# The last three feature tiles of an FFN down projection, column tile by column tile; two PSUM banks begun first instead of four

## The chip, the cores and the metric

The kernel runs on one NeuronCore of one Trainium2 chip. The metric is the device time of one execution in microseconds (us), as the median over several executions. A core has a matmul engine (PE in the profile), three engines for elementwise work (DVE, the vector engine; ACT, the scalar engine; POOL, GpSimd) and SP, an engine that does nothing here but issue DMAs. Each engine takes its instructions strictly in the order in which they stand in its own stream; an instruction that has to wait holds up everything behind it on its engine. That holds for SP too: a DMA whose buffer isn't free yet holds up the DMAs behind it. Matmul results go into eight accumulator banks (PSUM); everything else lies in on-chip buffers (SBUF).

## The reference

One layer of a decoder trunk: attention and a state space model side by side, an output projection, and a gated FFN with a short convolution, then a final norm. It is run on a prompt of 2048 tokens and on 8 samples of 4 tokens (2080 tokens together), all in float32. What matters here is the last part, with D_MODEL = 1024 and D_FF = 2688:

```python
def _conv_ffn(h, prev, w_up, conv_w, conv_b, w_down):
    up = h @ w_up
    buf = jnp.concatenate([prev.astype(up.dtype), up], axis=1)
    c = conv_b + sum(conv_w[i] * buf[:, i:i + L] for i in range(CONV_W))
    a, g = jnp.split(c, 2, axis=-1)
    return (jax.nn.silu(g) * a) @ w_down, buf[:, -(CONV_W - 1):]
...
    x = x + f
...
    y_prompt = _rmsnorm(xp, norm_final)
    y_sample = _rmsnorm(xs, norm_final)
```

The change touches the product with `w_down`, the addition of `x`, and the norm behind it.

## The kernel before

**Stages.** After the mixer the FFN runs twice, for two token groups (`gi` = 0 with tokens 0 to 1023, `gi` = 1 with 1024 to 2079). In each, 21 calls of `unit` make the up projection, convolution and gate of one feature tile of 128 features each and write the result, as a high and a low part, to a scratch array `actscr` in DRAM. Then `down(gi, beside)` multiplies with `w_down`. `down` of group 0 is followed by the units of group 1.

**Tiles of down.** `TILESD` cuts group 0 into two token tiles of 512 and group 1 into three of 448, 352 and 256. Tiles are named here by their first token: 0, 512, 1024, 1472, 1824. For each, the output is 8 column tiles `m` of 128 columns, each accumulated in a PSUM bank of its own (`dn_<tile>_<m>`), over 21 feature tiles `f`. One pass of the loop handles one feature tile for all 8 columns. The inner step `one(i, m)` is `mm3`, three matmuls into bank m: high weights by high activations (L89), high weights by low activations (L90), low weights by high activations (L91). So a pass is 24 matmuls and a token tile 504.

**Weights.** `load_wd` reads the 128 x 1024 weights of a feature tile from DRAM (`wdr`, L1457, two raw buffers for even and two for odd feature tiles). ACT then casts the high part (`wdh`, L83) and POOL makes the low part by subtraction (`wdl`, L84). `wdh` and `wdl` have three buffers each, so the split of one feature tile can't begin before the matmuls of the third last one have read theirs. The units share these buffers: their weights (`whv`/`wlv`, `whs`/`wls`, `whg`/`wlg`) rotate through the same three. In group 1 the first 14 feature tiles stay in SBUF (`wd`) for all three token tiles; the last two token tiles run through the features in the order 0, 1, 14, 2, 3, 15, ..., 12, 13, 20, so only every third pass needs a split.

**Activations.** `load_a` reads the two parts of a feature tile (`ah`, `al`, L1475) from `actscr`, up to three tiles ahead, into ten buffers that the norm's squares (`sq_fo`) share.

**The end of a token tile.** Behind the 21 passes stands, for each column, a DMA that reads `x` (`xo`, L1519) and a DVE addition of the bank to it (L1522). Then `finish` takes the squares on ACT (L130, L133), adds them up on DVE (`ss_fo`, L134), sums over partitions with a matmul (`st_fo`, L1437), and goes by ACT (L1440, L1441) and DVE (L1442 to L1444) to the scale, to the multiplication (L1447) and the write of the output (L1448). `finish` is a generator: its second part, from `st_fo` on, is emitted within the next token tile.

**Which banks start first.** At the start of a tile some banks are still read by earlier work. `behind` names the columns that are left out of the first `wait` passes and put into `late`; at pass `wait` the `st_fo` of the tile before and then the late steps are emitted. For the first tile of a group `behind` is (2, 3, 6, 7) and `wait` is 2, for the others (7,) and 3. Banks 0 to 3, 4 and 5, and 6 and 7 belong to three kinds of PSUM pools that the units use too.

**What sets the order.** The program is written once, and a scheduler puts each engine's instructions in order, by dependencies and priorities. SP's stream holds the weight loads, the `ah`/`al` loads, the `xo` loads and the output writes of all this.

Of the kernel before, what the change touches and what calls it, by code (L numbers as in the profile page):

```python
# [27 lines left out]
NF = DFF // P  # L28
# [11 lines left out]
TILES3 = [(260 * i, 260) for i in range(8)]  # L40
CB = 10
TILESD = [[(0, 512), (512, 512)], [(1024, 448), (1472, 352), (1824, 256)]]
DLATE, ULATE = 3, 2
YB = 1
FINLOW = -35
HP = 0
# [40 lines left out]
def mm3(nc, ps, w, x, first, last):  # L87

    nc.tensor.matmul(ps, w[0], x[0], start=first, stop=False)  # L89
    nc.tensor.matmul(ps, w[0], x[1], start=False, stop=False)  # L90
    nc.tensor.matmul(ps, w[1], x[0], start=False, stop=last)  # L91
# [565 lines left out]
def body(tc, a):  # L657
# [16 lines left out]
    with ExitStack() as top:  # L674
# [756 lines left out]
        def finish(t0, n, xs, first):  # L1431

            with after_preload() if first else nullcontext():
                ss = sumsq(c, DP, xs, n, f"fo_{t0}", nc.vector)
            yield
            ps = psv[1].tile([P, 512], F32, tag="u3", name=f"st_fo_{t0}")[:, :n]
            nc.tensor.matmul(ps, ones[1024], ss, start=True, stop=True)  # L1437
            r0 = DP.tile([P, n], F32, "ss", f"r0_fo_{t0}")
            r = DP.tile([P, n], F32, "rs", f"rs_fo_{t0}")
            nc.scalar.activation(r0, ps, AF.Ln, bias=c.eps)  # L1440
            nc.scalar.activation(r0, r0, AF.Exp, scale=-0.5)  # L1441
            nc.vector.scalar_tensor_tensor(r, ps, EPS, r0, ALU.add, ALU.mult)  # L1442
            nc.vector.scalar_tensor_tensor(r, r, -0.5, r0, ALU.mult, ALU.mult)
            nc.vector.scalar_tensor_tensor(r, r, 1.5, r0, ALU.add, ALU.mult)  # L1444
            for k, x in enumerate(xs):
                with tc.high_priority(offset=FINLOW):
                    nc.vector.scalar_tensor_tensor(x, x, g_fin[:, k : k + 1], r, ALU.mult, ALU.mult)  # L1447
                nc.sync.dma_start(yv[:, k, t0 : t0 + n], x)  # L1448
# [3 lines left out]
        def load_wd(gi, j, t0):  # L1452

            if j in wds:
                return wds[j]
            r = (sp if j % 2 else wp).tile([P, KD, P], F32, tag="wur", name=f"wdr_{t0}_{j}", bufs=2).rearrange("p k n -> p (k n)")
            nc.sync.dma_start(r, a["w_down"][j * P : j * P + P, :])  # L1457
            if gi and j < 14:
                if j in (4, 5):
                    w = [ffn.hc.tile([P, D], F32R, tag=f"t2{j - 4}{i}", name=f"wd{i}_{j}") for i in "hl"]  # L1460
                else:
                    i = j if j < 4 else j - 6
                    pl, nm = ((ha, "x0"), (hd, "q1"), (hb, "q0"))[0 if j < 4 else 1 + i // 4]
                    t = pl.tile([P, 2, D], F32R, tag=f"{nm}{i % 4 // 2}{'hl'[i % 2]}", name=f"wd_{j}")
                    w = [t[:, 0], t[:, 1]]
                wds[j] = w
            else:
                w = [wp.tile([P, KD, P], F32R, tag=f"wu{i}", name=f"wd{i}_{t0}_{j}", bufs=3).rearrange("p k n -> p (k n)") for i in "hl"]
            ffn.last_act, ffn.last_pool = split(nc, *w, r, nc.scalar, nc.gpsimd)
            return w  # L1470

        def load_a(j, t0, n):
            hl = [dt([P, n], F32R, f"a{i}_{t0}_{j}") for i in "hl"]
            for i, t in enumerate(hl):
                ffn.last_sp = nc.sync.dma_start(t.bitcast(F32), actscr[:, j, 1 - i, t0 : t0 + n]).ins  # L1475
            return hl

        def down(gi, beside):

            old = None  # L1480
            for ti, (t0, n) in enumerate(TILESD[gi]):
                xs, pts, ahl, late = [], {}, {}, []
                order = list(range(NF))
                if gi and ti:
                    order = [f for i in range(7) for f in (2 * i, 2 * i + 1, 14 + i)]

                def one(i, m):
                    if m not in pts:
                        pl, tag = ((psx, "ux"), (psu, "u2"), (psv[0], "u3"), (psv[1], "u3"))[max(0, m - 2) // 2 if m < 6 else m - 4]
                        pts[m] = pl.tile([P, 512], F32, tag=tag, name=f"dn_{t0}_{m}")  # L1490
                    mm3(nc, pts[m][:, :n], [w[:, m * P : m * P + P] for w in ahl[i][1]], ahl[i][0], i == 0, i == NF - 1)

                hls = {} if ti else ffn.first
                for i, j in enumerate(order):
                    for ahead in range(i, min(i + 3, NF)):
                        if ahead not in hls:
                            hls[ahead] = load_a(order[ahead], t0, n)
                    ahl[i] = hls[i], load_wd(gi, j, t0)
                    if ti == 0:
                        behind, wait = (2, 3, 6, 7), ULATE  # L1500
                    else:
                        behind, wait = (KD - 1,), DLATE
                    for m in range(KD):
                        if i < wait and m in behind:
                            late.append((i, m))
                        else:
                            if i == wait and late:
                                if old is not None:
                                    next(old, None)
                                for li, lm in late:  # L1510
                                    one(li, lm)
                                late = []
                            one(i, m)
                    if i > (0, 5)[ti > 0]:
                        with tc.issue_after(ffn.last_dve), tc.issue_after(ffn.last_act), tc.issue_after(ffn.last_pool), tc.issue_after(ffn.last_sp):
                            next(beside, None)
                for m in range(KD):
                    x = xp.tile([P, 2 * W], F32, tag="xo", name=f"xo_{t0}_{m}", bufs=8)[:, :n]
                    nc.sync.dma_start(x, x2scr[:, m, t0 : t0 + n])  # L1519
                    xs.append(x)  # L1520
                    with tc.high_priority(offset=HPD):
                        nc.vector.tensor_tensor(x, x, pts[m][:, :n], ALU.add)  # L1522
                old = finish(t0, n, xs, ti == 0)
                next(old)
            return old
# [17 lines left out]
        for gi in range(2):  # L1543
            ffn.first = {}
            for j in range(NF):
                if (gi, j) != (0, 0):
                    ws = load_wup(gi, j)
                unit(gi, j, ws, None if j or gi else finish_front, (last_norm if gi else None) if j == 0 else load_ahead if j == NF - 1 else None)
            beside = prepare(1) if gi == 0 else iter(())
            last = down(gi, beside)  # L1550
            for _ in beside:
                pass
# [125 lines left out]
```

## Time and profile before

| | us |
|---|---|
| median of 3 runs | 2178.76 (2177.89 to 2179.62) |
| the profiled execution, its own time | 2182.85 |
| span of the profile | 2180.4 |
| mean granted PE clock of the profiled execution | 0.976 |

The five token tiles of `down` stand in this execution at 1199.0, 1319.1, 1897.7, 2012.1 and 2101.1 us from the span's start (the first matmul of the tile, or where it would have come). The windows view gives for these stretches:

```profile
core 0: us, PE busy (x) PEld busy (x) DVE busy (x) ACT busy (x) POOL busy (x), PEclk, DMA share, GB/s
1199.00:1319.00 120.00, 118.50 (x506) 94.19 (x504) 58.20 (x83) 45.61 (x67) 63.94 (x32) 1.00 0.84 274
1319.00:1451.00 132.00, 123.00 (x510) 96.84 (x509) 38.74 (x39) 28.59 (x34) 58.80 (x27) 0.97 0.64 214
1897.70:2012.00 114.30, 107.39 (x506) 97.25 (x504) 12.59 (x28) 23.80 (x35) 39.08 (x17) 0.96 0.58 165
2012.00:2101.00 89.00, 84.14 (x508) 82.99 (x507) 18.97 (x27) 12.78 (x19) 17.34 (x7) 0.98 0.52 171
2101.00:2180.00 79.00, 62.38 (x510) 60.45 (x508) 24.49 (x46) 11.12 (x20) 12.43 (x5) 0.94 0.41 120
```

A row of this view is a stretch of time, its length, the busy time and the number of instructions of each engine, and PEclk, the mean clock granted to PE. A row of the timeline is the start, the duration (of several like instructions in a row, together), engine, line, operation and tiles; behind it in square brackets stands how long the engine had been idle before and what ended that (the releaser). A row of the view of waits is who waited for what: the sum in us, how many times, the longest.

### The profile page before, as it was taken

To read this page: it belongs to the slowest core of one execution; us is meant where nothing else is said; L and a number is where in the kernel's file an instruction comes from. 1 tells how busy PE (TensorE), PEld (TensorE's weight loads), DVE (VectorE), ACT (ScalarE), POOL (GpSimd) and SP (SyncE) were. 2 spreads that over 40 slices of the span, in tenths; PEclk is the share of its full clock that TensorE was granted. 3 is DMA by queue.
4 is the path that set the end of the run, shared out by engine and by line. 5 is a ranking of instruction groups with operands and counts; after the bars stand their busy time and mean duration, and the time that the engine had idled before them with its cause. 6 is when DMAs were issued, how large, how long until landed. Compare 5 with 4: busy or idle time off the path is not lost.

```text
span 2180.4 us, 41454 instructions
## 1 busy us (share of the span) xinstructions
PE 2051.2 (94%) x14685; PEld 1922.0 (88%) x14685; DVE 1297.7 (60%) x3295; ACT 1055.7 (48%) x2467; POOL 1217.6 (56%) x1199
## 2 busy tenths in 40 slices
PE   8989999978999979999999998999999999999997
PEld 7977878867999979999999786779999999888997
DVE  8849898368566576676766265246666666601231
ACT  6625554675444456666666332235665665612011
POOL 4777676334456766666665553455666666823120
PEclk9999999989999989999999999999999999999999
DMA  7854434786578733333334885924333333573643
GB/s 230 255 195 135 137 103 119 144 230 190 150 240 273 247 118 96 110 108 101 110 101 127 269 275 193 315 84 158 108 101 105 108 97 109 179 201 125 197 140 92
DMA packets 290319, 347.58 MB, mean 159 GB/s; under 512 B 41896, under 2 KB 246320, under 8 KB 289584
## 3 DMA queue, kind: packets, MB, share of 16 engines
q1 hardware_dynamic: 290112, 344.94, 51.7%
q8 instruction: 116, 1.90, 0.4%
q14 instruction: 91, 0.75, 0.1%
HBM read 232.70 MB, written 107.80 MB: 156 GB/s over the span
## 4 chain that ended last, share of the span: by engine, by line
PE 76%; DVE 7%; DMA 6%; POOL 5%; ACT 3%; issue 2%; SPq 1%; DVEq 0%; POOLq 0%; ACTq 0%
PE ux L1365 20%; PE u L1365 16%; PE dn L90 7%; PE dn L91 7%; PE dn L89 7%; PE wo L90 2%; PE wo L89 2%; PE wo L91 2%; PE qkv L89 2%; PE qkv L91 2%; PE qkv L90 2%; PE o L570 1%; DVE xo L1447 1%; DMA wdr<-in_w_down 1%; PE tp_b L559 1%
## 5 line engine op out<-in xcount | busy, mean ns | idle before, releaser
L84 POOL TENSOR_TENSOR wdl<-wdr,wdh 128x1024 fp32r<-128x1024 f32 x65 | 159.4, 2457 | 279.5 <-ACT wdh L83 242.4
L89 PE MATMUL dn<-ah,wdh 128*128 128x512 f32 (+3 forms) x552 | 204.4, 370 | 7.6 <-DMA ah<-actscr 3.6
L91 PE MATMUL dn<-ah,wdl 128*128 128x512 f32 (+3 forms) x552 | 203.7, 369 | 2.5 <-POOL wdl L84 2.5
L90 PE MATMUL dn<-al,wdh 128*128 128x512 f32 (+3 forms) x552 | 204.0, 370 | 0.7 <-DMA al<-actscr 0.7
L1330 ACT ACTIVATE cc<-u,cw 128x260 f32<-128x260 f32 (+1 forms) x252 | 141.5, 563 | 97.3 <-DVE u L1408 67.1
L1522 DVE TENSOR_TENSOR xo<-xo,dn 128x512 f32<-128x512 f32 (+3 forms) x40 | 21.9, 584 | 262.3 <-PE dn L91 262.2
L83 ACT CAST wdh<-wdr 128x1024 fp32r<-128x1024 f32 x65 | 68.1, 1050 | 224.9 <-PE dn L90 183.6
L84 POOL TENSOR_TENSOR wls<-s,whs 128x1024 fp32r<-128x1024 f32 x42 | 101.0, 2406 | 132.9 <-ACT whs L83 132.9
L1331 DVE SCALAR_TENSOR_TENSOR cc<-u,cw,cc 128x260 f32<-128x260 f32 (+1 forms) x252 | 121.1, 481 | 66.1 <-ACT cc L1330 64.6
L89 PE MATMUL wo<-mh,wo 128*128 128x260 f32 x512 | 148.4, 290 | 0.0
L90 PE MATMUL wo<-ml,wo 128*128 128x260 f32 x512 | 146.3, 286 | 0.1
L91 PE MATMUL wo<-mh,wo 128*128 128x260 f32 x512 | 146.2, 286 | 0.0
L1408 DVE TENSOR_TENSOR u<-u,cb 128x262 f32<-128x262 f32 x84 | 36.5, 435 | 159.2 <-PE u L1365 159.2
L89 PEld LDWEIGHTS dn<-ah,wdh 128*128 128x128 f32 x552 | 104.3, 189 | 27.1 <-issue 4.1
L84 POOL TENSOR_TENSOR wlt<-s,wht 128x512 fp32r<-128x512 f32 x42 | 54.1, 1288 | 124.7 <-ACT wht L83 60.1
L89 PE MATMUL qkv<-hh_p,wqh 128*128 128x256 f32 (+1 forms) x384 | 114.7, 299 | 8.1 <-DVE qs L900 3.6
L91 PEld LDWEIGHTS dn<-ah,wdl 128*128 128x128 f32 x552 | 104.4, 189 | 20.2 <-POOL wdl L84 3.7
L1332 DVE SCALAR_TENSOR_TENSOR cc<-u,cw,cc 128x260 f32<-128x260 f32 (+1 forms) x252 | 119.6, 475 | 0.8
L90 PEld LDWEIGHTS dn<-al,wdh 128*128 128x128 f32 x552 | 104.4, 189 | 17.4 <-DMA al<-actscr 1.2
L84 POOL TENSOR_TENSOR wlg<-wur,whg 128x1024 fp32r<-128x1024 f32 x42 | 101.1, 2407 | 30.3 <-ACT whg L83 30.3
L91 PE MATMUL qkv<-hh_p,wql 128*128 128x256 f32 (+1 forms) x384 | 111.4, 290 | 6.2 <-POOL wql L84 6.2
L90 PE MATMUL qkv<-hl_p,wqh 128*128 128x256 f32 (+1 forms) x384 | 111.3, 290 | 0.0
(575 smaller groups left out, 8333.9 us busy)
## 6 DMA issues: line engine op xcount, KB each, us to landing
actscr<-cc SPq DMA_DIRECT2D x168, 260.0 KB, 2.5
wur<-in_w_up SPq DMA_DIRECT2D x84, 512.0 KB, 3.5
wdr<-in_w_down SPq DMA_DIRECT2D x77, 512.0 KB, 3.5
x<-in_xT SPq DMA_DIRECT2D x56, 256.0 KB, 4.0
hs<-h2scr SPq DMA_DIRECT2D x44, 262.0 KB, 5.6
ah<-actscr SPq DMA_DIRECT2D x42, 256.0 KB, 5.3
al<-actscr SPq DMA_DIRECT2D x42, 256.0 KB, 4.7
mt<-mscr SPq DMA_DIRECT2D x16, 520.0 KB, 6.3
```

Of the source, the lines that this page charges most:

```text
L83: i = nc.scalar.copy(hi, src) if hi_eng is nc.scalar else hi_eng.tensor_copy(hi, src)
L84: return i.ins, lo_eng.tensor_tensor(lo, src, hi.bitcast(F32), ALU.subtract).ins
L89: nc.tensor.matmul(ps, w[0], x[0], start=first, stop=False)
L90: nc.tensor.matmul(ps, w[0], x[1], start=False, stop=False)
L91: nc.tensor.matmul(ps, w[1], x[0], start=False, stop=last)
L559: nc.tensor.transpose(tp[:, P * j : P * j + P], ss[kv][:, j, P * ch : P * ch + P], c.ident)
L1330: nc.scalar.activation(cp, pp[:, 2:], AF.Identity, bias=w[3], scale=w[2])
L1331: nc.vector.scalar_tensor_tensor(cp, pp[:, 1 : npr + 1], w[1], cp, ALU.mult, ALU.add)
L1332: nc.vector.scalar_tensor_tensor(cp, pp[:, 0:npr], w[0], cp, ALU.mult, ALU.add)
L1365: nc.tensor.matmul(pt[:, :W], x[p][:, k], y[q][:, k], start=start and k + i == 0, stop=k == 3 and i == 2, skip_group_check=True)
L1408: v.tensor_tensor(c21[s], c21[s], cb[s][:, 0], ALU.add)
L1522: nc.vector.tensor_tensor(x, x, pts[m][:, :n], ALU.add)
```

## The change

For the last three feature tiles of every token tile (`MOUT` = 3) the inner step isn't emitted in the loop. It is put into `tail`, and behind the loop it comes column by column: for each column the steps of the three feature tiles, then the `xo` load and the addition. For the first token tile of a group, columns 4 and 5 join the late ones, so only banks 0 and 1 are begun in the first two passes; among the late steps those of columns 4 and 5 come first.

```diff
--- before.py
+++ after.py
@@ -40,7 +40,7 @@
 TILES3 = [(260 * i, 260) for i in range(8)]
 CB = 10
 TILESD = [[(0, 512), (512, 512)], [(1024, 448), (1472, 352), (1824, 256)]]
-DLATE, ULATE = 3, 2
+DLATE, ULATE, MOUT = 3, 2, 3
 YB = 1
 FINLOW = -35
 HP = 0
@@ -1491,13 +1491,14 @@
                     mm3(nc, pts[m][:, :n], [w[:, m * P : m * P + P] for w in ahl[i][1]], ahl[i][0], i == 0, i == NF - 1)
 
                 hls = {} if ti else ffn.first
+                tail = []
                 for i, j in enumerate(order):
                     for ahead in range(i, min(i + 3, NF)):
                         if ahead not in hls:
                             hls[ahead] = load_a(order[ahead], t0, n)
                     ahl[i] = hls[i], load_wd(gi, j, t0)
                     if ti == 0:
-                        behind, wait = (2, 3, 6, 7), ULATE
+                        behind, wait = (2, 3, 4, 5, 6, 7), ULATE
                     else:
                         behind, wait = (KD - 1,), DLATE
                     for m in range(KD):
@@ -1507,14 +1508,19 @@
                             if i == wait and late:
                                 if old is not None:
                                     next(old, None)
-                                for li, lm in late:
+                                for li, lm in sorted(late, key=lambda x: x[1] not in (4, 5)):
                                     one(li, lm)
                                 late = []
-                            one(i, m)
+                            if i < NF - MOUT:
+                                one(i, m)
+                            else:
+                                tail.append((m, i))
                     if i > (0, 5)[ti > 0]:
                         with tc.issue_after(ffn.last_dve), tc.issue_after(ffn.last_act), tc.issue_after(ffn.last_pool), tc.issue_after(ffn.last_sp):
                             next(beside, None)
                 for m in range(KD):
+                    for _, i in sorted(t for t in tail if t[0] == m):
+                        one(i, m)
                     x = xp.tile([P, 2 * W], F32, tag="xo", name=f"xo_{t0}_{m}", bufs=8)[:, :n]
                     nc.sync.dma_start(x, x2scr[:, m, t0 : t0 + n])
                     xs.append(x)
```

The lines behind move by six: the `xo` load is now L1525 and the addition L1528. The number of instructions stays the same on every engine.

On PE, at the end of token tile 0 (`dn_0_0` is column 0, `ah_0_18` the activations and `wdh_0_18`, `wdl_0_18` the weights of feature tile 18), before, feature tile 18 goes through the columns:

```order
L89 MATMUL dn_0_0_17266<-ah_0_18_17936,wdh_0_18_18034 128x512
L90 MATMUL dn_0_0_17266<-al_0_18_17937,wdh_0_18_18034 128x512
L91 MATMUL dn_0_0_17266<-ah_0_18_17936,wdl_0_18_18035 128x512
L89 MATMUL dn_0_1_17270<-ah_0_18_17936,wdh_0_18_18034 128x512
L90 MATMUL dn_0_1_17270<-al_0_18_17937,wdh_0_18_18034 128x512
L91 MATMUL dn_0_1_17270<-ah_0_18_17936,wdl_0_18_18035 128x512
L89 MATMUL dn_0_2_17320<-ah_0_18_17936,wdh_0_18_18034 128x512
```

Now column 0 takes feature tiles 18, 19 and 20 in a row, then column 1 begins:

```order
L89 MATMUL dn_0_0_17266<-ah_0_18_17936,wdh_0_18_18034 128x512
L90 MATMUL dn_0_0_17266<-al_0_18_17937,wdh_0_18_18034 128x512
L91 MATMUL dn_0_0_17266<-ah_0_18_17936,wdl_0_18_18035 128x512
L89 MATMUL dn_0_0_17266<-ah_0_19_17982,wdh_0_19_18050 128x512
L90 MATMUL dn_0_0_17266<-al_0_19_17983,wdh_0_19_18050 128x512
L91 MATMUL dn_0_0_17266<-ah_0_19_17982,wdl_0_19_18051 128x512
L89 MATMUL dn_0_0_17266<-ah_0_20_18028,wdh_0_20_18066 128x512
L90 MATMUL dn_0_0_17266<-al_0_20_18029,wdh_0_20_18066 128x512
L91 MATMUL dn_0_0_17266<-ah_0_20_18028,wdl_0_20_18067 128x512
L89 MATMUL dn_0_1_17270<-ah_0_18_17936,wdh_0_18_18034 128x512
```

The first reader of the low weights of feature tile 20 moves from 51 rows to 9 rows behind the start of feature tile 18 (counting that as the first), and the last reader of feature tile 18's weights, in column 7, moves to the last nine matmuls of the tile.

On ACT, where token tile 0 ends and 512 begins (`wdh_512_0` to `wdh_512_2` are casts of the next tile's weights, `ss_fo_0` and `sq_fo_0` squares of tile 0's output). Before:

```order
L672 ACT_TABLE_LOAD
L83 CAST wdh_512_0_18214<-wdr_512_0_18212 128x1024
L83 CAST wdh_512_1_18252<-wdr_512_1_18250 128x1024
L130 ACTIVATE ss_fo_0_18177<-xo_0_0_18152 128x512
L133 ACTIVATE sq_fo_0_0_18179<-xo_0_1_18155 128x512
L133 ACTIVATE sq_fo_0_1_18182<-xo_0_2_18158 128x512
L133 ACTIVATE sq_fo_0_2_18185<-xo_0_3_18161 128x512
L133 ACTIVATE sq_fo_0_3_18188<-xo_0_4_18164 128x512
L83 CAST wdh_512_2_18283<-wdr_512_2_18281 128x1024
L133 ACTIVATE sq_fo_0_4_18191<-xo_0_5_18167 128x512
```

Now:

```order
L672 ACT_TABLE_LOAD
L130 ACTIVATE ss_fo_0_18177<-xo_0_0_18089 128x512
L133 ACTIVATE sq_fo_0_0_18179<-xo_0_1_18101 128x512
L133 ACTIVATE sq_fo_0_1_18182<-xo_0_2_18113 128x512
L133 ACTIVATE sq_fo_0_2_18185<-xo_0_3_18125 128x512
L133 ACTIVATE sq_fo_0_3_18188<-xo_0_4_18137 128x512
L133 ACTIVATE sq_fo_0_4_18191<-xo_0_5_18149 128x512
L83 CAST wdh_512_0_18214<-wdr_512_0_18212 128x1024
L133 ACTIVATE sq_fo_0_5_18194<-xo_0_6_18161 128x512
L83 CAST wdh_512_1_18252<-wdr_512_1_18250 128x1024
L83 CAST wdh_512_2_18283<-wdr_512_2_18281 128x1024
L133 ACTIVATE sq_fo_0_6_18197<-xo_0_7_18173 128x512
```

The casts of the next tile's first two feature tiles have moved from ahead of the squares to behind the sixth and seventh of them.

On SP at the same place (`wdr_512_4`, `wdr_512_5` are raw weights, `ah_512_0` and `al_512_0` the first activations that tile 512 needs). Before:

```order
L1457 DMA wdr_512_4_18381<-in_w_down 128x1024
L1457 DMA wdr_512_5_18415<-in_w_down 128x1024
L1475 DMA ah_512_0_18200<-actscr_65 128x512
L1475 DMA al_512_0_18201<-actscr_65 128x512
L1475 DMA ah_512_1_18204<-actscr_65 128x512
L1475 DMA al_512_1_18205<-actscr_65 128x512
```

Now:

```order
L1457 DMA wdr_512_4_18381<-in_w_down 128x1024
L1475 DMA ah_512_0_18200<-actscr_65 128x512
L1475 DMA al_512_0_18201<-actscr_65 128x512
L1475 DMA ah_512_1_18204<-actscr_65 128x512
L1475 DMA al_512_1_18205<-actscr_65 128x512
L1475 DMA ah_512_2_18208<-actscr_65 128x512
L1475 DMA al_512_2_18209<-actscr_65 128x512
L1475 DMA ah_512_3_18246<-actscr_65 128x512
L1475 DMA al_512_3_18247<-actscr_65 128x512
L1475 DMA ah_512_4_18277<-actscr_65 128x512
L1475 DMA al_512_4_18278<-actscr_65 128x512
L1457 DMA wdr_512_5_18415<-in_w_down 128x1024
```

The load of `wdr_512_5` has moved behind ten loads of activations; that of `wdr_512_4` still stands ahead of them. Where tile 1024 ends and 1472 begins, `wdr_1472_19` moves in the same way behind the activations, and `wdr_1472_18` stays ahead.

## The prediction

> **What bounds the kernel now.** I read the page first, for which engine carries the time, then PE's waits in the stretches of `down`, then the timeline of PE, ACT, POOL, SP and DVE at the places where the change moves something. The page's busy time and its chain:
>
> ```profile
> PE 2051.2 (94%) x14685; PEld 1922.0 (88%) x14685; DVE 1297.7 (60%) x3295; ACT 1055.7 (48%) x2467; POOL 1217.6 (56%) x1199
> PE 76%; DVE 7%; DMA 6%; POOL 5%; ACT 3%; issue 2%; SPq 1%; DVEq 0%; POOLq 0%; ACTq 0%
> ```
>
> PE is busy 94% of the span and holds 76% of the chain that ended last. The matmuls stay the same in number and size, so the change is worth only what it does to PE's idle gaps in and around `down`, and to the end behind the last matmul. So I count gaps: how late each thing that PE needs comes, in matmuls ahead of the end T of a tile.
>
> **Part 1: the weights of the last feature tile, +7.5.** The last three passes of tiles 0, 512 and 1024 in PE's timeline (first matmul S, and for two tiles the last), then the cast and the low part of feature tile 20 on ACT and POOL:
>
> ```profile
> 1302.30 0.40 PE L89 MATMUL dn<-ah,wdh 128*128 128x512 f32 x1
> ...
> 1318.88 0.40 PE L91 MATMUL dn<-ah,wdl 128*128 128x512 f32 x1
> ...
> 1434.06 0.40 PE L89 MATMUL dn<-ah,wdh 128*128 128x512 f32 x1
> ...
> 1997.47 0.37 PE L89 MATMUL dn<-ah,wdh 128*128 128x448 f32 x1
> ...
> 2011.85 0.37 PE L91 MATMUL dn<-ah,wdl 128*128 128x448 f32 x1
> 1304.27 1.04 ACT L83 CAST wdh<-wdr 128x1024 fp32r<-128x1024 f32 x1
> 1434.07 1.05 ACT L83 CAST wdh<-wdr 128x1024 fp32r<-128x1024 f32 x1 [4.58 <-PE dn L90]
> 1305.61 2.40 POOL L84 TENSOR_TENSOR wdl<-wdr,wdh 128x1024 fp32r<-128x1024 f32 x1
> 1435.20 2.40 POOL L84 TENSOR_TENSOR wdl<-wdr,wdh 128x1024 fp32r<-128x1024 f32 x1 [3.23 <-ACT wdh L83]
> 1998.64 2.40 POOL L84 TENSOR_TENSOR wdl<-wdr,wdh 128x1024 fp32r<-128x1024 f32 x1 [2.53 <-ACT wdh L83]
> ```
>
> From S to the last matmul are 71 steps: 16.58 / 71 = 0.2335 us each in a 512 tile, 14.38 / 71 = 0.2025 in the 448 tile. T is one step behind: 1319.11 and 2012.05. The cast at 1434.07 was released by PE: feature tile 20 takes the buffer of feature tile 17, whose last reader is the pass that ends at S. So the split of tile 20 can't start earlier than now, and it ends at 1305.61 + 2.40 = 1308.01, at 1437.60 and at 2001.04. Before, it was wanted two passes behind S. Now the ninth matmul behind S wants it, at S + 8 steps: 1304.17, 1435.93 and 1999.09. PE waits 3.84 + 1.67 + 1.95 = 7.5. Nothing hides this, since PE has nothing else in its stream there. In tiles 1472 and 1824 feature tile 20 takes the buffer of the pass nine places ahead: 0. In tile 0 ACT began the cast 1.9 behind its release (1304.27, where tile 512 has S + 0.01), behind other work in its stream; if that came sooner, the wait would be 1.9 instead of 3.84. That stream stays the same there, so I keep 3.84.
>
> **Part 2: the start of tiles 512 and 1472, +2.4 and +3.8.** The end of tile 0: the next tile's casts and low parts, SP's issues, and PE's first two matmuls of tile 512; then SP and PE where 1024 ends, and where 1472 ends:
>
> ```profile
> 1311.28 1.05 ACT L83 CAST wdh<-wdr 128x1024 fp32r<-128x1024 f32 x1
> 1312.41 4.78 POOL L84 TENSOR_TENSOR wdl<-wdr,wdh 128x1024 fp32r<-128x1024 f32 x2 [4.39 <-ACT wdh L83]
> 1308.04 0.33 SPq L1457 DMA_DIRECT2D wdr<-in_w_down  x1
> 1308.47 4.10 SPq L1519 DMA_DIRECT2D xo<-x2scr  x8
> 1314.84 2.71 SPq L1457 DMA_DIRECT2D wdr<-in_w_down  x2
> 1317.64 0.39 SPq L1475 DMA_DIRECT2D ah<-actscr  x1
> 1322.93 0.46 PE L89 MATMUL dn<-ah,wdh 128*128 128x512 f32 x1 [3.65 <-DMA ah<-actscr]
> 1991.27 19.82 SPq L1457 DMA_DIRECT2D wdr<-in_w_down  x5
> 2011.14 0.42 SPq L1475 DMA_DIRECT2D ah<-actscr  x1
> 2014.73 0.40 PE L89 MATMUL dn<-ah,wd 128*128 128x352 f32 x1 [2.51 <-DMA ah<-actscr]
> 2101.12 0.32 SPq L1475 DMA_DIRECT2D al<-actscr  x1
> 2103.25 0.39 PE L90 MATMUL dn<-al,wd 128*128 128x256 f32 x1 [1.89 <-DMA al<-actscr]
> ```
>
> SP issues the weight loads of the next tile ahead of its `ah`, and the raw buffer of `wdr_512_4` comes free only when POOL has split `wdl_512_0`. That split needs the buffer of feature tile 18. Its last reader moves from the end of a pass (T less two passes, 11.2) to 8 steps ahead of T. PE's release reaches ACT 0.48 behind the matmul's start (for the cast at 1434.07 that matmul stood two steps ahead of S, at 1433.59). So: cast from T - 1.87 + 0.48 = T - 1.39 to T - 0.34; POOL 0.08 later and 2.40 long, to T + 2.14; SP 0.03 later the weight load and 0.43 behind it `ah` (1308.01, 1308.04 and 1308.47 show both steps), at T + 2.60. Before it was 1317.64, T - 1.47. The landing took 5.29 here (behind eight `xo` loads and two weight loads), 3.59 at 2011.14 (behind one weight load), 2.13 at 2101.12 (nothing ahead). Now the `xo` loads are long done and one weight load is just ahead, as at 2011.14, so I take 3.59: PE starts at T + 6.19 in place of T + 3.82, **+2.4** (bounds by the other two landings +0.9 and +4.1). Tile 1472 in the same way, with 8 steps of 0.2025: cast T - 1.14 to T - 0.09, POOL to T + 2.39, `ah` at T + 2.85, PE at T + 6.44 in place of T + 2.68: **+3.8** (+2.3 to +5.5). The loads of `wdr_512_5` and `wdr_1472_19` are moved past ten activation loads; they are wanted passes later, so 0. The table load and the squares now ahead of the casts end before the casts' release, so 0.
>
> **Part 3: the start of unit(1, 0), +1.2.** The cast, the low part, and PE at the end of tile 512:
>
> ```profile
> 1439.67 1.05 ACT L83 CAST whv<-wur 128x1024 fp32r<-128x1024 f32 x1 [4.55 <-PE dn L90]
> 1444.90 2.40 POOL L84 TENSOR_TENSOR wlv<-wur,whv 128x1024 fp32r<-128x1024 f32 x1
> 1450.86 0.28 PE L1365 MATMUL ux<-x00h,whv 128*128 128x262 f32 x1
> ...
> 1451.10 0.29 PE L1365 MATMUL ux<-x00h,wlv 128*128 128x262 f32 x1
> 1462.11 1.12 PE L1437 MATMUL st_fo<-ss_fo,ones 128*128 128x512 f32 x2 [0.69 <-DVE ss_fo L134]
> 1466.11 0.39 PE L1365 MATMUL u<-q11h,whs 128*128 128x262 f32 x1 [2.88 <-DVE rs_fo L1442]
> ```
>
> Here the next work takes the same weight buffers. `wlv` comes at T + 2.14 as in part 2, the third matmul wanted it at T + 0.24: +1.9. The sums on DVE now run while columns finish, so the 0.69 ahead of `st_fo` goes: together **+1.2**. The wait of 2.88 behind it follows `st_fo` and moves along. The value isn't seen directly; it is at best -0.7 (the later wait swallows the first) and at worst +1.9.
>
> **Part 4: what it gains, -3.4.** At T of tile 1472 the `al` load (2101.12) waited for the buffer of feature tile 20, read last two steps ahead of T. It now takes that of feature tile 12, the first of the three in column 7, read last eight steps ahead: six steps of 0.2025 x 352 / 448 = 0.16 make **-0.9** of the 1.89 (0 to -1.89). The end of the kernel:
>
> ```profile
> 2163.58 2.90 DVE L1522 TENSOR_TENSOR xo<-xo,dn 128x256 f32<-128x256 f32 x8 [43.10 <-PE dn L91]
> 2166.40 3.59 DVE L134 TENSOR_TENSOR ss_fo<-ss_fo,sq_fo 128x256 f32<-128x256 f32 x7
> 2170.05 1.22 PE L1437 MATMUL st_fo<-ss_fo,ones 128*128 128x256 f32 x2 [4.02 <-DVE ss_fo L134]
> ```
>
> Seven sums of 0.51 stand behind the additions. Six of them now run earlier, but the last still needs the last column's square on ACT, some 0.45 behind its addition: 6 x 0.51 less 0.6 for that and the hand-overs gives **-2.5** (from -1.5, if sums still bunch, to -3.1). Nothing is late behind it that wasn't: the chain from `st_fo` on is the same.
>
> **Part 5: fewer banks at the start, 0.** PE's waits there, and the DVE operations that free banks 2 and 3 in group 1:
>
> ```profile
> PE dn L89 <- DVE cc L1350: 6.9, 4, 3.5
> PE dn L89 <- DVE cc L1350: 1.5, 3, 0.8
> 1907.83 0.43 DVE L1350 TENSOR_TENSOR cc<-ux,cc 128x260 fp32r<-128x260 f32 x1 [2.48 <-ACT cc L1349]
> 1912.17 0.43 DVE L1350 TENSOR_TENSOR cc<-ux,cc 128x260 fp32r<-128x260 f32 x1 [1.04 <-ACT cc L1349]
> ```
>
> Group 1 waits 6.9 in four pieces, group 0 1.5 in three. The two pieces at banks 4 and 5 get smaller, but banks 2 and 3 are free at 1908.3 and 1912.6 whatever PE did ahead, so the saved time is waited there: 0. At best the pieces at banks 4 and 5, at most 3.9 of both groups by these sums, really go; PE can't lose here.
>
> **Part 6: the clock behind new waits, +1.6.** In tile 512 and in tile 1472:
>
> ```profile
> 1326.86 0.40 PE L91 MATMUL dn<-ah,wdl 128*128 128x512 f32 x1
> 2018.33 0.49 PE L89 MATMUL dn<-ah,wd 128*128 128x352 f32 x1
> 2019.71 0.32 PE L91 MATMUL dn<-ah,wd 128*128 128x352 f32 x1
> ```
>
> Behind the 3.65 gap eight steps took 3.93, 0.44 of it a wait; at 0.2335 they take 1.87, so the slow stretch cost 1.6. Behind the 2.51 gap matmuls of the same form lasted 0.49 against 0.32 later. Of the new waits only that of tile 0 (3.84) is as long, so I add 1.6 once; its bounds are 0 and four times that.
>
> The Trainium skill, in "TensorE: Matmul & The Clock Gate", Part 1, says that PE falls to half clock after at least one idle window of about 3.4 us. The slow rows behind 2.51 show that here less is enough. By the rule the wait of tile 0 would cost no clock, since two matmuls cut it into pieces below 3.4 (L89 waits for the cast until 1305.3, L91 for POOL until 1308.0), and the sum would be 1.6 less, 2190.3.
>
> **Sum.** 7.5 + 2.4 + 3.8 + 1.2 - 3.4 + 0 + 1.6 = +13.1. The profiled execution took 2182.85 (span 2180.4), so 2196.0 on its scale; it was 4.1 above the median of the runs, 2178.76, which gives **2191.9**.
>
> **Rivals.**
> - *Short waits*: the cast in tile 0 comes at its release, loads land in 2.13, part 3 is swallowed, no clock is lost: 5.6 + 0.9 + 2.3 - 0.7 - 3.4 = +4.7, 2183.5. For: less is in flight. Against: the 3.59 behind one weight load. 0.10.
> - *The start gains*: banks 4 and 5 cost no wait and nothing takes its place: 13.1 - 3.9 = +9.2, 2188.0. Against: DVE's rows in part 5. 0.10.
> - *Both*: +0.8, 2179.6, no change. 0.05.
> - *All waits at their worst*: 7.5 + 4.1 + 5.5 + 1.9 - 3.4 + 6.4 = +22.0, 2200.8. For: the slow rows behind 2.51. 0.08.
> - *Faster: the split isn't behind PE.* If the weights of feature tile 20 are ready 8 steps behind S, ahead of their buffer's last reader now, parts 1 and 2 are 0 and the gains stay: -0.7 - 3.4 - 1.0 (the start of group 0) = -5.1, 2173.7. It decides from the point where `wdl` of tile 20 ends by 1304.2 in place of 1308.0. Against: the cast's releaser in part 1 is PE, three buffers deep, and the change adds no buffer. 0.07. That the change doesn't do what it says is the same case seen from its start: it brings the columns to their ends one by one, as it says, but what follows is bound elsewhere.
>
> **How the numbers follow.** My forecast has 0.60. Within 0.2% (4.4 us, about what a measurement of this kernel can tell from no change) is 2174.4 to 2183.1: 0.05. Faster 0.07, slower 0.88. The range of 2182 to 2199 takes in the bounds of parts 2, 3 and 6; it leaves out the faster case, the unchanged one and the far end of the worst.
>
> **What would show it.** Three gaps ahead of L91 or L89 in the first column of the last three feature tiles, of 3.8, 1.7 and 2.0, ended by ACT or POOL; gaps of 6 at the starts of 512 and 1472 ended by `ah`; a gap of 1.9 at the third matmul of unit(1, 0); the last `st_fo` 2.5 sooner behind the last `dn` matmul; the sum of the start waits as before. It is wrong if the first three gaps aren't there, or if the starts of 512 and 1472 are no later than before.

## The result, and the profile after

| | before | after |
|---|---|---|
| median, us | 2178.32 (2177.10 to 2179.62, 4 runs) | 2194.78 (2191.37 to 2197.32, 4 runs) |
| ratio | | 1.0062 (95% interval 1.0040 to 1.0083) |
| span of the profiled execution | 2180.4 | 2195.2 |

The changed kernel is slower by 0.62%, 13.5 us by the ratio (8.7 to 18.1); the two medians lie 16.5 apart. The forecast was 13.1 more, 2191.9. The page after:

```profile
PE 2050.5 (93%) x14685; PEld 1918.8 (87%) x14685; DVE 1299.0 (59%) x3295; ACT 1057.5 (48%) x2467; POOL 1218.9 (56%) x1199
```

PE does the same work. From the first matmul of tile 0 on, the changed kernel takes 12.9 us longer; by PE's busy time in the windows view 2.6 of them are slower matmuls (6.5 more in `down`, 3.9 less in the units of group 1), the rest is idle time. First, PE's waits from tile 0 to unit(1, 0), in the view of waits of the changed kernel:

```profile
PE dn L91 <- POOL wdl L84: 7.0, 4, 2.1
PE dn L89 <- DMA ah<-actscr: 6.2, 1, 6.2
PE dn L89 <- ACT wdh L83: 3.0, 2, 2.0
...
PE ux L1365 <- POOL wlv L84: 1.8, 1, 1.8
```

Before, the same stretch waited 2.5, 3.6 and 0.2 for the first three, and not at all for the fourth. Then the gaps one by one, with their neighbours where the clock matters, from PE's timeline of the changed kernel:

```profile
1307.79 0.49 PE L89 MATMUL dn<-ah,wdh 128*128 128x512 f32 x1 [1.96 <-ACT wdh L83]
...
1310.61 0.79 PE L91 MATMUL dn<-ah,wdl 128*128 128x512 f32 x1 [2.09 <-POOL wdl L84]
...
1311.63 0.63 PE L90 MATMUL dn<-al,wdh 128*128 128x512 f32 x1
1312.06 0.63 PE L91 MATMUL dn<-ah,wdl 128*128 128x512 f32 x1
...
1333.39 0.76 PE L89 MATMUL dn<-ah,wdh 128*128 128x512 f32 x1 [6.17 <-DMA ah<-actscr]
...
1340.97 0.44 PE L89 MATMUL dn<-ah,wdh 128*128 128x512 f32 x1
...
1451.74 0.50 PE L91 MATMUL dn<-ah,wdl 128*128 128x512 f32 x1 [1.52 <-POOL wdl L84]
...
1468.87 0.39 PE L1365 MATMUL ux<-x00h,wlv 128*128 128x262 f32 x1 [1.76 <-POOL wlv L84]
1482.21 0.39 PE L1365 MATMUL u<-q11h,whs 128*128 128x262 f32 x1 [2.16 <-DVE rs_fo L1442]
1497.29 0.40 PE L1365 MATMUL u<-x00h,whv 128*128 128x262 f32 x1 [1.62 <-DVE cc L1350]
...
2011.44 0.47 PE L91 MATMUL dn<-ah,wdl 128*128 128x448 f32 x1 [1.75 <-POOL wdl L84]
2031.11 0.63 PE L89 MATMUL dn<-ah,wd 128*128 128x352 f32 x1 [6.34 <-DMA ah<-actscr]
2047.28 0.43 PE L89 MATMUL dn<-ah,wd 128*128 128x352 f32 x1 [1.99 <-DVE rs_fo L1442]
...
2121.16 0.39 PE L90 MATMUL dn<-al,wd 128*128 128x256 f32 x1 [1.00 <-DMA al<-actscr]
2185.42 0.70 PE L1437 MATMUL st_fo<-ss_fo,ones 128*128 128x256 f32 x2 [1.48 <-DVE ss_fo L134]
```

Every gap that the forecast named is there: three in the first column of the tails (that of tile 0 in two pieces), 6.2 and 6.3 at the starts of 512 and 1472, 1.8 at the third matmul of unit(1, 0), and the two shorter ones at the end. How far the changed kernel is behind, at the same matmul of both timelines, tells where the time went:

| at the first matmul of | before | after | behind | change since the row above | forecast |
|---|---|---|---|---|---|
| tile 0 | 1199.00 | 1200.94 | 1.9 | 1.9 (code that is the same in both) | 0 |
| unit(1, 0) | 1450.86 | 1466.70 | 15.8 | +13.9 | +9.5 (part 3's wait comes behind this matmul) |
| tile 1024 | 1897.74 | 1907.48 | 9.7 | -6.1 | +1.2 |
| tile 1472 | 2014.73 | 2031.11 | 16.4 | +6.6 | +5.8 |
| tile 1824 | 2101.09 | 2119.89 | 18.8 | +2.4 | 0 |
| the last st_fo | 2170.05 | 2185.42 | 15.4 | -3.4 | -3.4 |

So the sum was met, but two of its pieces were wrong and nearly cancel: the second and the fifth row lost 6.8 more than forecast, and the units of group 1 (the third row) were 7.3 us faster than forecast.

### The profile page after: what moved, and what is told of

The parts are those of the page before. It is cut to its first block, busy times and chain, and to the rows that moved or that the text cites. A ratio compares the mean times of both kernels' runs of the same rounds, so it can differ in the third digit from the quotient of the medians.

```text
span 2195.2 us, 41436 instructions
## 1 busy us (share of the span) xinstructions
PE 2050.5 (93%) x14685; PEld 1918.8 (87%) x14685; DVE 1299.0 (59%) x3295; ACT 1057.5 (48%) x2467; POOL 1218.9 (56%) x1199
## 5 line engine op out<-in xcount | busy, mean ns | idle before, releaser
L1528 DVE TENSOR_TENSOR xo<-xo,dn 128x512 f32<-128x512 f32 (+3 forms) x40 | 23.3, 584 | 245.8 <-PE dn L91 243.0
L90 PEld LDWEIGHTS dn<-al,wdh 128*128 128x128 f32 x552 | 105.2, 191 | 18.1 <-DMA al<-actscr 1.5
L89 PE MATMUL dn<-ah,wd 128*128 128x448 f32 (+2 forms) x288 | 96.9, 336 | 18.0 <-DVE cc L1350 8.0
```

## The experiments

All eight are the changed kernel with edits, five rounds each beside the kernel before, whose median was 2182.5 in the first four and 2182.8 in the others. They share this edit, which sets the depth of the tail for each token tile (one line more, so lines from there on are one higher):

```diff
-DLATE, ULATE, MOUT = 3, 2, 3
+DLATE, ULATE = 3, 2
+MOUT = {...}
-                            if i < NF - MOUT:
+                            if i < NF - MOUT[t0]:
```

All but the first also begin four banks as before:

```diff
-                        behind, wait = (2, 3, 4, 5, 6, 7), ULATE
+                        behind, wait = (2, 3, 6, 7), ULATE
```

The question of the first four is which part of the change costs what.

**Only the start with two banks.**

```diff
+MOUT = {0: 0, 512: 0, 1024: 0, 1472: 0, 1824: 0}
```

> Only the second part of the change: banks 0 and 1 alone are begun in the first two passes of a group, no tail. My theory (the time is lost in the tails, where PE waits for the split weights of the last feature tile, and at the tile starts behind them; banks 2 and 3 come free at times that DVE sets, so the start only moves its waits): within 1 us of before, about +0.5, since the two start waits of the changed kernel's profile are 0.5 longer in each group. Rival (beginning only two banks carries the loss): +10 to +16 us, and the tail-only kernel is near before.

Measured: ratio 1.0007 (0.9995 to 1.0019), +1.5 us (-1.1 to +4.1). Its waits for DVE at the two starts, in the view of waits:

```profile
PE dn L90 <- DVE cc L1351: 1.9, 2, 1.4
...
PE dn L90 <- DVE cc L1351: 8.3, 3, 3.6
```

Fewer and longer waits than before (1.5 in three, 6.9 in four), with sums 0.4 and 1.4 larger. The start doesn't carry the loss.

**Only the tail, in all tiles.**

```diff
+MOUT = {0: 3, 512: 3, 1024: 3, 1472: 3, 1824: 3}
```

> Only the first part: the tail of three feature tiles in all five token tiles, four banks begun as before. My theory: +11 to +14 us, with PE waits of about 4.0, 1.6 and 1.8 in the first column of the tails of tiles 0, 512 and 1024, ended by ACT or POOL, and waits of about 6.2 for ah at the starts of tiles 512 and 1472. Rival (the two-bank start carries the loss): near before.

Measured: 1.0056 (1.0038 to 1.0073), +12.2 us (8.3 to 15.9). The gaps on PE's timeline:

```profile
1306.70 0.50 PE L90 MATMUL dn<-ah,wdh 128*128 128x512 f32 x1 [1.49 <-ACT wdh L84]
...
1309.54 0.80 PE L92 MATMUL dn<-ah,wdl 128*128 128x512 f32 x1 [2.11 <-POOL wdl L85]
1332.28 0.76 PE L90 MATMUL dn<-ah,wdh 128*128 128x512 f32 x1 [6.26 <-DMA ah<-actscr]
...
2026.40 0.63 PE L90 MATMUL dn<-ah,wd 128*128 128x352 f32 x1 [6.43 <-DMA ah<-actscr]
```

The same gaps as with the whole change, the ones in tiles 512 and 1024 too (1.51 and 1.75). Within the intervals the tail carries the whole loss, 12.2 of 13.5.

**A tail of two feature tiles.**

```diff
+MOUT = {0: 2, 512: 2, 1024: 2, 1472: 2, 1824: 2}
```

> A tail of two feature tiles instead of three in all five token tiles, start as before. Feature tile 20 is then wanted one pass and five matmuls behind the release of its buffer (5.6 + 1.2 = 6.8 us in a 512 tile, where the split took 5.7 and 3.5), so my theory says that the waits in the first column go to 0 in all tiles. The start of tiles 512 and 1472 stays late, since the second weight load ahead of ah now hangs on the last columns: ah issued about 3.3 behind the tile's end, PE waits there 6 to 7. Sum against before: 0 for the tails, +3 and +4.4 at the two starts, about +2 of slow clock behind them, -0.9 and -2 for the last two tiles, and 0 to -6 where unit(1, 0) begins: +1 to +7. Rival (the column order itself is slow, whatever the weights): the three waits or a like loss remain, +9 or more.

Measured: 1.0012 (1.0000 to 1.0024), +2.6 us (0 to 5.2). No gap stands in the first column of any tail; the late starts remain:

```profile
1328.52 0.77 PE L90 MATMUL dn<-ah,wdh 128*128 128x512 f32 x1 [8.25 <-DMA ah<-actscr]
...
2023.29 0.63 PE L90 MATMUL dn<-ah,wd 128*128 128x352 f32 x1 [6.89 <-DMA ah<-actscr]
```

So it isn't the column order that is slow. With the weights of the last feature tile in time, 9.6 us of the 12.2 are gone; the waits in the three first columns (1.49 + 2.11, 1.51 and 1.75 with the tail of three, 6.9 together) and the slow clock behind the first of them are of that size. The profiled executions lie 6.5 apart in span, less than the medians: the units of group 1 took 444.3 us here and 440.7 with the tail of three.

**The tail of three only in the last two tiles.**

```diff
+MOUT = {0: 0, 512: 0, 1024: 0, 1472: 3, 1824: 3}
```

> The tail of three feature tiles only in the last two token tiles (1472 and 1824), whose last feature tile's weights are split passes ahead. My theory: no wait in the tails, the start of 1824 earlier by 0.9, the last st_fo 2.5 sooner behind the last dn matmul: -2.5 to -4 us against before. Rival (a column-wise tail costs by itself, or the end is bound by something else): 0 or slower.

Measured: 0.9975 (0.9963 to 0.9988), -5.5 us (-8.1 to -2.6), and so faster than before. In these tiles the last feature tile's weights are split long ahead, and the tail shows no wait. Its two gains:

```profile
2106.57 0.39 PE L91 MATMUL dn<-al,wd 128*128 128x256 f32 x1 [0.87 <-DMA al<-actscr]
...
2170.82 0.70 PE L1438 MATMUL st_fo<-ss_fo,ones 128*128 128x256 f32 x2 [1.48 <-DVE ss_fo L135]
```

Before, these waits were 1.89 and 4.02. The gaps account for 3.6; the measured 5.5 has an interval that holds both.

**The tail only in tile 512.** This asks where the 6.1 us in the units of group 1 came from.

```diff
+MOUT = {0: 0, 512: 3, 1024: 0, 1472: 0, 1824: 0}
```

> The tail of three only in token tile 512, start as before. In the changed kernel the stretch from the end of tile 512 to the start of tile 1024 was 6.1 us shorter than before, where my prediction had +1.2. Theory: it comes from the sums of tile 512's squares, which now run while columns end, so that DVE reaches the scaling of the tile earlier against GpSimd's weight work; then it stays when only this tile has a tail, and the kernel is +1.7 (wait for feature tile 20) -6 = about -4 us, -2 to -6. Rival (chance of how the two engines meet, caused by the delays ahead): about +1.7 + 1.2 = +3, 0 to +4.

Measured: 0.9999 (0.9988 to 1.0010), -0.2 us (-2.6 to +2.2): between the two, and the time alone settles nothing. The profiles show more. The next fences show the eight scalings (L1447, in experiments L1448) of tile 512's output on DVE, GpSimd's work beside them, and the wait of PE that follows; first the kernel before:

```profile
1468.88 1.65 DVE L1447 SCALAR_TENSOR_TENSOR xo<-xo,vec,rs_fo 128x512 f32<-128x512 f32 x1
1470.80 8.67 DVE L1447 SCALAR_TENSOR_TENSOR xo<-xo,vec,rs_fo 128x512 f32<-128x512 f32 x7
1469.95 2.85 POOL L84 TENSOR_TENSOR wlv<-wur,whv 128x1024 fp32r<-128x1024 f32 x1
1485.27 0.59 PE L1365 MATMUL u<-x00h,whv 128*128 128x262 f32 x1 [4.21 <-DVE cc L1350]
```

The changed kernel:

```profile
1483.64 0.75 DVE L1447 SCALAR_TENSOR_TENSOR xo<-xo,vec,rs_fo 128x512 f32<-128x512 f32 x1
1484.65 6.85 DVE L1447 SCALAR_TENSOR_TENSOR xo<-xo,vec,rs_fo 128x512 f32<-128x512 f32 x7
1485.01 2.63 POOL L84 TENSOR_TENSOR wlv<-wur,whv 128x1024 fp32r<-128x1024 f32 x1 [3.12 <-ACT whv L83]
```

The tail in tile 512 alone, and PE's wait with the start of two banks alone:

```profile
1470.96 0.75 DVE L1448 SCALAR_TENSOR_TENSOR xo<-xo,vec,rs_fo 128x512 f32<-128x512 f32 x1
1472.32 6.86 DVE L1448 SCALAR_TENSOR_TENSOR xo<-xo,vec,rs_fo 128x512 f32<-128x512 f32 x7
1485.93 0.39 PE L1366 MATMUL u<-x00h,whv 128*128 128x262 f32 x1 [1.45 <-DVE cc L1351]
```

```profile
1483.80 0.39 PE L1366 MATMUL u<-x00h,whv 128*128 128x262 f32 x1 [1.44 <-DVE cc L1351]
```

The scalings take 10.3 us in the kernel before, 7.6 in the two with a tail in tile 512, and 8.2 with the start alone (1.65 for the first and 6.50 for the others). In the kernel before three of the eight are long: the first lasts 1.65, beside GpSimd work, the second, beside `wlv`, 2.56, and the last, beside `wls`, 2.88, where one alone lasts 0.74. In the changed kernel one is long, 2.87 beside `wlv`. With the tail PE's wait goes from 4.2 to 1.6 and 1.5, and the slow clock that followed the long wait doesn't come.

The stretch from unit(1, 0) to tile 1024 lasted 446.9 before and 447.0 in the kernels with a tail in the last two tiles only, with and without the early load below; 440.7 to 443.6 in the five with a tail of three in tile 512; but also 442.8 with the start alone, which has no tail anywhere, and 444.3 with the tail of two, where two scalings were long and PE's wait was 5.2. The larger part of the difference is the clock: of the 6.1 us between the kernel before and the changed one PE's waits in the stretch make 2.2 (9.4 against 7.2), and its busy time for the same matmuls 3.9 (437.5 against 433.6; the granted clock is 0.5 during 10.2 us of the stretch before and nowhere in it after). So the gain depends on how the two engines meet and on whether the clock falls behind the waits; a tail of three in tile 512 brought it each time, and it comes without one too. That the sums' earlier end is its cause isn't shown.

**The first activations of the next tile early.** In the next three, `ah` and `al` of the next tile's first feature tile are loaded with the last feature tile, and so stand on SP ahead of the weight loads:

```diff
-                hls = {} if ti else ffn.first
+                hls = nxt if ti else ffn.first
+                nxt = {}
...
                     ahl[i] = hls[i], load_wd(gi, j, t0)
+                    if i == NF - 1 and ti + 1 < len(TILESD[gi]):
+                        nxt[0] = load_a(0, *TILESD[gi][ti + 1])
```

With the tail of three in all tiles:

> The tail of three in all token tiles, start as before, and the first ah and al of the next token tile are loaded at the last feature tile, so they stand on SP ahead of the weight loads that wait for GpSimd. Theory (the late start of tiles 512 and 1472 is SP's queue: ah stands behind a weight load that waits for a split that waits for the last columns): the waits of 6.2 and 6.3 for ah vanish; behind them remain about 1.7 for the low weights of tile 512's first feature tile and 1 to 3 for the second ah. Against the tail-only kernel 10 to 14 us less, so -2 to +3 us against before. Rival (the loads land late because of traffic, or the weights set the start anyway): as late as the tail-only kernel, +9 to +13.

Measured: 1.0013 (1.0003 to 1.0023), +2.8 us (0.7 to 5.0), 9.4 less than the tail alone, just short of the 10 that I expected at least. What is left of the 6.3 and 6.4:

```profile
1328.76 0.50 PE L92 MATMUL dn<-ah,wdl 128*128 128x512 f32 x1 [1.51 <-POOL wdl L85]
...
2024.05 0.66 PE L90 MATMUL dn<-ah,wd 128*128 128x352 f32 x1 [3.08 <-DMA ah<-actscr]
```

The start of tile 512 now waits for its first low weights, that of 1472 in the second pass for the second `ah`, which still stands behind a weight load. The first `ah` is no longer waited for in either place, so the late start was SP's order, not the landing.

With the tail only in tiles 1472 and 1824:

> The same early load of the first ah and al, and the tail of three only in tiles 1472 and 1824. The waits for ah and al at the starts of tiles 512, 1472 and 1824 (3.65 + 0.44, 2.51 + 0.36 and 1.9 in before) should vanish, with the slow clock behind the first two (1.8 and 1.9), and the end stays 2.5 sooner: -5 for the last tiles as measured, and -7 to -11 for the starts, so -11 to -16 us against before. Rival (the second ah or the weights come late instead): -5 to -8.

Measured: 0.9953 (0.9938 to 0.9967), -10.3 us (-13.5 to -7.2). The view of waits, from tile 1024 on:

```profile
PE dn L90 <- DVE cc L1351: 6.7, 4, 3.2
PE dn L90 <- DVE rs_fo L1443: 3.7, 2, 2.0
PE st_fo L1438 <- DVE ss_fo L135: 1.5, 1, 1.5
PE dn L91 <- DMA al<-actscr: 0.3, 1, 0.3
```

No wait for `ah` is left and 0.3 for `al`; before there were 2.5 and 2.5. These waits vanished as expected. The gain lies just short of the low end of what I expected, 11: at the start of tile 512 the 3.6 for `ah` is gone too, but the waits for weights from tile 0 to unit(1, 0) grew from 2.7 to 4.1, which the expected sum leaves out.

With the tail in tile 512 as well:

> As the kernel with the early load and the tail in tiles 1472 and 1824, and tile 512 has the tail too. If the shorter stretch behind tile 512 comes from its tail: 2 to 6 us less than without it. If it was chance: 0 to 4 us more.

Measured: 0.9945 (0.9927 to 0.9962), -12.0 us (-15.9 to -8.3). The wait in the tail is there (1.51), and the stretch of units is short (440.8). Against the kernel without it that is 1.7 less by the medians of ratios, but the intervals overlap widely; the two are not told apart. Both are faster than the kernel before and the changed one.

## Why the prediction was right, point by point

- **Part 1, the weights of feature tile 20 (+7.5): right.** The waits in the three tails were 1.96 + 2.09, 1.52 and 1.75, together 7.3, ended by ACT or POOL as named. The tail of two, with the split in time, shows that the lack of time is the cause, and the last two tiles show none.
- **Part 2, the starts of 512 and 1472 (+2.4, +3.8): right.** The waits grew by 2.5 and 3.8. The landing behind one weight load, taken as 3.59, was 3.8 both times. The early load took the waits away, which shows that SP's queue held `ah` back.
- **Part 3, the start of unit(1, 0) (+1.2): wrong.** Its two waits were right: 1.76 for `wlv`, and the 0.69 went. The step that failed is "the wait of 2.88 behind it follows `st_fo` and moves along", and with it everything behind: I held DVE's pace and the clock fixed. That wait fell to 2.16, the scalings took 7.6 instead of 10.3, the wait for the last of DVE's chain fell from 4.21 to 1.62, and the slow clock, 3.9 us of PE's busy time, didn't come. The stretch was 6.1 shorter, outside even the bound of -0.7.
- **Part 4, the gains (-3.4): right**, -0.9 and -2.5 as the gaps of 1.00 and 1.48 show.
- **Part 5, the start (0): right** within what is measured (+1.5, -1.1 to +4.1).
- **Part 6, the clock (+1.6): right that clock is lost, wrong in size.** For the same matmuls PE's busy time in `down` rose from 494.0 to 500.5 us (from tile 0 to unit(1, 0), and from tile 1024 to the last `st_fo`), so the clock cost 6.5 more than before. I counted one new slow stretch. It came, half speed behind the two pieces in tile 0 (1311.63 to 1312.06 is 0.43 a step, against 0.2335). But the slow stretches that were there before also got longer: in tile 512 half speed lasts until 1340.97, 7.6 behind the first matmul, where it was 3.9; at the start of tile 1472 it lasts 6.3, where it was 3.4; and behind the 1.99 wait in tile 1472 there is one of 3.7 that wasn't there before. The length of a single wait was the wrong measure, as the last section shows. The Trainium skill's rule, as the prediction read it (pieces below 3.4 cost no clock), would have been further off. The Trainium skill's sentence that the window runs free, in the same part of "TensorE: Matmul & The Clock Gate", fits: in each trace all changes of the granted clock lie on one grid of 3.41 us, and the grid lies elsewhere in each execution.
- Rows that I didn't count: the later waits for weights in tile 512 grew (7.0 for POOL and 3.0 for ACT in the stretch, of which the tails are 5.6, so 4.4 against 2.7 before).

The total was right partly by luck: parts 1, 2, 4 and 5 were right, and the error of part 3 (-7.3) nearly cancels those of part 6 (+4.9) and the later waits (+1.7).

## What to carry to other kernels

Bringing columns to their ends early pays only where the last weights are ready a whole tail ahead: compare the time from the release of a rotating buffer to its next use with the time of the split, and give the reordered tail only to the tiles that have the slack. Before reordering readers, look for what is queued behind the buffers that they now hold longer; here a load whose buffer was free waited on SP behind one whose buffer was not, and moving it ahead took 9.4 us off the kernel with tails in all tiles. Where two engines slow each other and the clock falls behind the waits, a shift ahead of them moves time by several us either way (440.7 to 447.0 for the same stretch here), so a term for it needs a wide bound on both sides. What a wait costs in clock depends on how much of a 3.41 us window it leaves idle, and so on where the window's edges fall, which differs from execution to execution.

## What the hardware showed that was not expected

DVE and GpSimd slow each other, but not for every operation. The views of the lines of the scaling, the sum of squares and the addition of a bank around the end of tile 512 (shortest, median and longest in ns, first and last start), of the kernel before:

```profile
L1447 DVE SCALAR_TENSOR_TENSOR xo<-xo,vec,rs_fo x8: 740/742/2879, 1468.9 to 1476.6; 128x512 f32<-128x512 f32 x8
```

and of the changed kernel:

```profile
L134 DVE TENSOR_TENSOR ss_fo<-ss_fo,sq_fo x7: 692/1216/2039, 1455.8 to 1470.7; 128x512 f32<-128x512 f32 x7
L1528 DVE TENSOR_TENSOR xo<-xo,dn x8: 673/680/686, 1452.3 to 1469.3; 128x512 f32<-128x512 f32 x8
```

The scaling and the sum read two operands in SBUF and take up to four and three times their shortest; GpSimd's `wlv` beside them took 2.85 against 2.40. The Trainium skill's "GPSIMD Engine Reference", section 1, says that the two engines share their way into SBUF, with contention where the DVE instruction has two SBUF inputs; the rows agree: the addition, which reads one operand from PSUM, stayed at 0.67 to 0.69 among them.

Half speed of PE comes in whole windows of 3.41 us, and it goes with PE's idle time within a window, not with the length of one wait. The same wait of 1.99 in tile 1472 shows it. In the kernel before, an edge between two windows cuts the wait in two, and no half speed follows; in the changed kernel the wait lies within one window, and it does. In the windows view (behind the stretch and its length stands PE's busy time; the clock is the third figure from the end), the first two rows are of the kernel before, the others of the changed one:

```profile
2026.42:2029.83 3.41, 1.64 (x8) 0.92 (x6) 0.45 (x1) 1.21 (x2) 0.00 (x0) 1.00 0.00 0
2029.83:2033.24 3.41, 3.18 (x20) 3.19 (x21) 3.31 (x7) 1.05 (x1) 0.41 (x1) 1.00 0.42 120
2044.20:2047.61 3.41, 1.42 (x7) 0.70 (x6) 0.98 (x2) 1.21 (x2) 0.00 (x0) 1.00 0.00 0
2047.61:2051.02 3.41, 3.41 (x14) 3.41 (x13) 3.34 (x7) 0.92 (x1) 0.00 (x0) 0.50 0.56 154
```

Counted from tile 0 to 2165 us in all ten traces: of the windows at full speed, all 55 in which PE was busy for less than 0.44 of the window were followed by one at half speed, and none of the 2663 with more than 0.51; between the two both occurred. A window at half speed was followed by another one as long as PE was busy for 0.82 of it or less (all 30), and by full speed from 0.83 on (all 62). That is why half speed lasted longer behind the later start of tile 512. For tile 0 it is the window from 1306.92 to 1310.33, which holds parts of both pieces: PE was busy for 0.73 of its 3.41 us.
